# A transformer layer on one core: four of the seven operand sums of the down projection made one stage earlier and stored, the rest moved to VectorE

## The chip, the core and the metric

One core of a Trainium2 chip runs the whole kernel. The metric is the device time in microseconds (us), the median of three timed runs; lower is better. The engines of the core are TensorE (PE, with its weight load PEld), VectorE (DVE), ScalarE (ACT), GpSimd (POOL) and SyncE (SP), which here only issues DMA transfers.

## The reference

The kernel computes one layer of a hybrid encoder in float32 on 1024 tokens with 1024 features: attention and a recurrence side by side, an output projection, and then a SwiGLU block with 2816 hidden features (22 tiles of 128). Only the last line matters here:

```
h2 = rmsnorm(x, norm2_g[l])
x = x + (jax.nn.silu(h2 @ w_gate[l]) * (h2 @ w_up[l])) @ w_down[l]
```

The stage that makes silu(h2 @ w_gate) * (h2 @ w_up) is called the gate/up stage below, and its result g (2816 x 1024). The product g @ w_down is the down stage.

## The kernel before

**Products.** A float32 product runs as three passes: each operand is the exact sum of two rounded parts h and l, and PE adds h*h, l*h and h*l. An operand is split by one ACT instruction (h, a cast, L72) and one DVE instruction (l, a subtraction, L73), each on 128x512 elements. Both stages use Strassen's scheme in Winograd's form: the left matrix A and the right matrix B are cut into 2 x 2 blocks, and seven products P1 to P7 stand in for eight. Some of their operands are sums of blocks: S1 = A21 + A22, S2 = S1 - A11, S3 = A11 - A21, S4 = A12 - S2, T1 = B12 - B11, T2 = B22 - T1, T3 = B22 - B12, T4 = B21 - T2.

**Gate/up stage.** After a first pair of hidden tiles, which is multiplied plainly (`classic`; its products land in g by the DVE instruction of L942), 20 steps follow, g1, u1, g2, ... u10, two for each of ten pairs of hidden tiles. A step is an object `Step`: it has 7 products of 12 matmuls (L931, tiles Pg and Pu). Its `run` calls `after(i)` behind product i, and that makes the operand i of the next step (`make`: the S sums on POOL at L1060 to L1063, then the split on ACT and DVE). Results leave PSUM through ACT copies and DVE additions (L1091, L1102, L1111). Each finished tile of g is stored to DRAM by `spill` (L923, one 512 KB transfer on SP). The weights come by `load_raw` (L901, 512 KB each, tiles graw and uraw). Four PSUM banks serve the g steps and four the u steps, in turn, so a product waits until the result four products before it in its step has been read.

**Down stage.** The list PRODUCTS gives the order of the seven products: P1 (A11, B11), P2 (A12, B21), P7 (S3, T3), P5 (S1, T1), P6 (S2, T2), P3 (S4, B22), P4 (A22, T4). A is g and B is w_down. Each has 11 positions of 12 matmuls (L1334, tile P), 77 slots of 12 matmuls in all. Operand tiles are named by slot and side: d371l is the l part of slot 37's right operand. The splits run two slots ahead (AHEAD = 2). The raw blocks are loaded by `load_d` (L1168), first from within the last step by `end_step`, then by a list of loads behind it. The table SUMS says which engine makes which sum and where it is put: all S sums on POOL, all T sums on DVE (both L1189), each called by `sum_of` from the loop over the slots. A sum takes the place of a block that is not needed any more. At the ends of the products, DVE adds the PSUM banks to running values (L1341) and ACT copies others out. `add` joins values in SBUF, 28 times, on POOL (L1276). The results go out by L1212.

**Order.** A scheduler puts each engine's instructions in a row, and each engine runs its row in that order, waiting at the head for whatever the instruction needs. The order of a row is therefore what the text speaks of.

Of the kernel before, what the change touches and what calls it, by code (L numbers as in the profile page):

```python
# [9 lines left out]
F32 = mybir.dt.float32  # L10
# [24 lines left out]
def hymba_layer(ctx: ExitStack, tc: tile.TileContext, x, norm1_g, w_in, q_norm_g, k_norm_g, b_f,  # L35
                conv_w, conv_b, w_a, b_a, w_x, b_x, lam, attn_out_g, lru_out_g, w_out, norm2_g,
                w_gate, w_up, w_down, out):
    """Float32 products run as three float32r passes: an operand is the exact sum h + l of two
    float32r values (12 bits each), and h*h + h*l + l*h carries the float32 product."""
# [71 lines left out]
    # the gain on all partitions  # L111
# [54 lines left out]
        # nlc = 4 softplus(-lam), so that tanh(nlc * r) = tanh(-log_a / 2)  # L166
# [17 lines left out]
    def atanh(p_t, z, n):  # L184
        """p_t = atanh(z) for |z| <= 1/3"""
# [18 lines left out]
    # hT[half] = (h, l), each [feature, chunk of features, 512 tokens]  # L204
# [36 lines left out]
    def prep(p):  # L241
        """q and k of two heads, feature-major, as h and l"""
# [13 lines left out]
    def load_max(h):  # L256
        """what the maxima need"""
# [13 lines left out]
    def max_steps(h):  # L271
# [18 lines left out]
        def rows(half):  # L290
            # -max of 512 queries, turned into a row of QB
# [21 lines left out]
    with tc.tile_pool(name="pp", bufs=1) as pp:  # L313
# [36 lines left out]
        def proj_A(c, groups, evac, hooks=()):  # L350
            """psum[channel, token] for 128 channels and n tokens from t0 each; groups of (t2, t0, n)"""
# [15 lines left out]
        def proj_B(c, blocks, n, evac, *tags, hooks=()):  # L367
            """psum[token, column] for 128 tokens each"""
# [39 lines left out]
        # block-diagonal gate weights  # L408
# [32 lines left out]
        def lru_gates(t):  # L441
            """the four pieces of the gates"""
# [14 lines left out]
        def lru(t):  # L457
# [3 lines left out]
            # With t = tanh(-log_a / 2): a = 2 / (1 + t) - 1 and sqrt(1 - a^2) = 2 sqrt(t) / (1 + t).  # L461
            # 1 / (1 + t) = (1 + a) / 2 starts from a = exp(log_a) and takes a Newton step.
# [10 lines left out]
            # here i = -u: the scan runs on -h  # L473
# [61 lines left out]
        def log_f():  # L535
            # -log f = max(-z, 0) + log1p(exp(-|z|)) with exp(-|z|) = (1 - t) / (1 + t), t = tanh(|z| / 2)
# [190 lines left out]
    def spread(p, heads):  # L727
        """the inverse denominators of the heads of a pair, on their features"""
# [34 lines left out]
    # the recurrent half of the output projection, in pieces of 128 tokens by 256 columns  # L763
# [28 lines left out]
    # by head: pieces of the output projection, steps that the product with v lags, steps over which the other work is  # L792
    # spread, and the places of vprep and finish_pair in it
# [60 lines left out]
    def mm_out(groups):  # L854
        """psum += att @ w_out for groups of (psum, block, half), one chunk of features after the other"""
# [10 lines left out]
    # Strassen's scheme in Winograd's form, on two tiles of ff by two halves of d (weights: A) and two halves of d by  # L866
    # two halves of the tokens (B): seven products in place of eight. The sums S, T are float32, then split.
    #   S1 = A21 + A22, S2 = S1 - A11, S3 = A11 - A21, S4 = A12 - S2
    #   T1 = B12 - B11, T2 = B22 - T1, T3 = B22 - B12, T4 = B21 - T2
    #   u1 = A11 B11 + S2 T2, u2 = u1 + S3 T3  # L870
    #   C11 = A11 B11 + A12 B21, C12 = u1 + S1 T1 + S4 B22, C21 = u2 + A22 T4, C22 = u2 + S1 T1
    NPR = NFT // 2
    gz = ctx.enter_context(tc.tile_pool(name="gz", bufs=1))
    # a block's h and l: [tile of chunks 0 and 1, tile of chunks 2 and 3], [P, 2, 512] each
# [76 lines left out]
    with tc.tile_pool(name="nz", bufs=1) as nz:  # L951
# [37 lines left out]
        # the order of what follows: products of the first pair of ff tiles, plainly (g, u), the sums (tc, t3), their  # L989
        # splits (s3, t4), the loads (rw) and operands (mk) of the next pair  # L990
# [11 lines left out]

    T1 = slots4("q", "T1")
# [7 lines left out]
    def minus(eng, x, y, u):  # L1011
        """u = x - y of two split blocks"""
# [4 lines left out]
    def minus_sum(eng, x, t, u):  # L1017
        """u = x - t of a split block and a sum"""
# [30 lines left out]
    class Step:  # L1049
        """one weight matrix on one pair of ff tiles; operands in the order of the products"""  # L1050
# [23 lines left out]
        def run(self, after):  # L1074
# [9 lines left out]
            def result(i, j, x, y, tmp):  # L1084
                """the block x + y of the product, into silu(gate) or silu(gate) * up"""
# [48 lines left out]
    # The same scheme over tokens (A: g, two halves of the tokens by two times eleven tiles of ff) and columns  # L1134
    # (B: w_down). A sum takes the place of an operand that is not needed any more:
    #   S1 in A21, S2 in S1, S4 in A12, T1 in B12, T2 in T1, T4 in B21
    ND = NFT // 2
    UNITS = {"hA": 8, "hC": 8, "hB": 4, "hD": 4, "hE": 4, "hF": 4}
    raw = {}

    def places(*tags):
        """places of [P, 512] in slots"""
# [11 lines left out]
    def load_d(nm, k0, pl):  # L1154
        """blocks k0.. of A11, B21 and the like into places, a transfer for those side by side"""
        i, j = int(nm[1]) - 1, int(nm[2]) - 1
        while pl:
# [4 lines left out]
            if nm[0] == "A":  # L1162
# [14 lines left out]
    SUMS = {"S3": (pool, "sub", "A11", "A21", None), "T3": (dve, "sub", "B22", "B12", None),  # L1177
            "S1": (pool, "add", "A21", "A22", "A21"), "T1": (dve, "sub", "B12", "B11", "B12"),
            "S2": (pool, "sub", "A21", "A11", "A21"), "T2": (dve, "sub", "B22", "B12", "B12"),
            "S4": (pool, "sub", "A12", "A21", "A12"), "T4": (dve, "sub", "B21", "B12", "B21")}  # L1180
    sum_d, src_d, ops_d = {}, {}, {}

    def sum_of(nm, k):
        if nm not in SUMS:
            return raw[nm, k]
        if (nm, k) not in sum_d:
            eng, op, x_, y_, to = SUMS[nm]
            u = raw[to, k] if to else temp(f"{nm}{k}")
            (eng.tensor_add if op == "add" else eng.tensor_sub)(out=u, in0=raw[x_, k], in1=raw[y_, k])  # L1189
# [26 lines left out]
    def end_step(i):  # L1216
# [20 lines left out]
        elif i == 5:  # L1237
            load_d("B12", 0, places("r0", "r1", "r2", "r3"))
# [3 lines left out]
    for k, st in enumerate(steps):  # L1242
        def after(i):
            if k + 1 < len(steps):
# [14 lines left out]
    load_x2(0, 0, four)  # L1259
    load_d("A21", 0, places("hA"))  # L1260
    load_d("B22", 0, places("s0", "s1", "s2", "s3"))
    load_d("A21", 8, places("x0"))
    load_d("B12", 8, places("x1"))
    load_d("B22", 8, hb[:3])
    load_d("A21", 10, hb[3:])
    load_d("B12", 10, hf[:1])
    load_d("A22", 0, [(sq2, 1)])
# [7 lines left out]
    def add(x_, b, y_):  # L1275
        pool.tensor_add(out=at(x_, b), in0=at(x_, b), in1=at(y_, b))  # L1276

    for n, (nm, a_, b_, pos) in enumerate(dsteps):
# [4 lines left out]
        if n + AHEAD > 2:  # L1283
            for i in range(2):
                operand(n + AHEAD, i)
        if nm == "P7":
            if pos:
                sum_of("T1", pos - 1)
            if pos in (2, 4, 6):
                load_d("A22", pos - 1, places({2: "v0", 4: "v1", 6: "x2"}[pos]))  # L1290
            if pos == 10:
                load_d("A22", 7, places("hD"))
# [78 lines left out]
```

## Time and profile before

| | us |
|---|---|
| device time, median of 3 runs (lowest, highest) | 1208.71 (1208.33, 1208.89) |
| span of the profiled execution | 1207.5 |
| down stage: first to last matmul in that span | 958 to 1203.7 |
| the 20 steps g1 to u10: first to last matmul | 570 to 958 |

No device time of the profiled execution itself is on record; its span is 1.2 us below the median of the runs, and sums below are made as differences against the span and carried to the median. PE is busy 96% of the span, DVE 68%, ACT 43%, POOL 28%, and the 16 DMA engines move 101 GB/s on the mean. In the page's table of 40 slices of 30 us each, PE's share falls below 9 tenths late in the program:

```profile
PE   8999999999999989999899999999999999877998
DVE  6427759768887676768655545555455567999694
POOL 2000010031010210146442433424232013586390
PEclk9999999999999899999999999999999999889999
```

Each digit is the busy share of one slice in tenths; PEclk is the clock that TensorE was granted, in tenths of full speed.

### The profile page before, as it was taken

Reading aid. Unit: us, or ns where it says so; the run is one execution under the profiler, and the core shown is the slowest. Engines: PE = TensorE matmul, PEld = TensorE weight load, DVE = VectorE, ACT = ScalarE, POOL = GpSimd, SP = SyncE. Lnnn points to the kernel's source line nnn. Section 1 sums busy time; section 2 is a strip of 40 time slices with the busy share of each in tenths; the row PEclk is TensorE's granted clock in tenths of the full one; section 3 lists DMA queues with packets and bytes.
Section 4 is the critical chain, followed back from the end, with each engine's and each line's share of the span. In section 5 each row is a group of like instructions: output and inputs, shape, how many; then the busy total and the mean of one; then the engine's idle time right before and its main releaser. Section 6 shows DMA issues by size and latency. Waiting matters only on the chain.

```text
span 1207.5 us, 16502 instructions
## 1 busy us (share of the span) xinstructions
PE 1153.9 (96%) x6137; PEld 972.7 (81%) x6137; DVE 817.8 (68%) x1285; ACT 519.6 (43%) x931; POOL 342.1 (28%) x264
## 2 busy tenths in 40 slices
PE   8999999999999989999899999999999999877998
PEld 7988999987887777777788888888888887655876
DVE  6427759768887676768655545555455567999694
ACT  7437775325555453523333333333333344323432
POOL 2000010031010210146442433424232013586390
PEclk9999999999999899999999999999999999889999
DMA  6111111146565566521323123231223891200302
GB/s 245 28 53 45 36 36 36 30 91 147 154 154 138 143 173 190 179 88 35 114 70 105 53 87 92 91 105 53 87 87 122 315 329 54 71 0 1 105 27 79
DMA packets 82650, 122.21 MB, mean 101 GB/s; under 512 B 12097, under 2 KB 55209, under 8 KB 82570
## 3 DMA queue, kind: packets, MB, share of 16 engines
q1 hardware_dynamic: 82570, 121.16, 33.3%
q8 instruction: 48, 0.79, 0.3%
q14 instruction: 32, 0.26, 0.1%
HBM read 80.34 MB, written 24.21 MB: 87 GB/s over the span
## 4 chain that ended last, share of the span: by engine, by line
PE 72%; DVE 17%; DMA 3%; issue 3%; POOL 2%; ACT 2%; SPq 0%; POOLq 0%; DVEq 0%; ACTq 0%
PE Pu L931 16%; PE Pg L931 16%; PE P L1334 9%; PE pag L361 4%; PE pbk L377 4%; PE pbv L377 4%; PE pax L361 4%; PE pbq L377 3%; PE o L698 3%; PE fl L783 3%; DVE dr L1189 2%; DMA rb<-rd 2%; PE mx L284 1%; DVE dhC L1189 1%; PE st L676 1%
## 5 line engine op out<-in xcount | busy, mean ns | idle before, releaser
L684 ACT ACTIVATE pt<-st 128x512 f32<-128x512 f32 (+1 forms) x96 | 47.9, 508 | 52.3 <-PE st L679 27.4
L689 DVE TENSOR_TENSOR ringl<-pt,ringh 128x512 fp32r<-128x512 f32 (+2 forms) x96 | 58.2, 621 | 7.0 <-ACT ringh L686 5.6
L287 DVE TENSOR_REDUCE nm<-mx 128x1 f32<-128x512 f32 (+2 forms) x96 | 51.2, 549 | 13.6 <-PE mx L286 7.5
L783 PE MATMUL fl<-worec,rech 128*128 128x256 f32 x256 | 54.6, 295 | 1.1 <-DVE ql L76 0.7
L480 POOL TENSOR_TENSOR sqR<-sqR,i 128x1024 f32<-128x1024 f32 x3 | 7.2, 2400 | 150.8 <-ACT i L479 150.8
L1091 DVE TENSOR_TENSOR g<-pug,Pg 128x512 f32<-128x512 f32 x30 | 20.6, 687 | 39.2 <-PE Pg L931 39.2
L783 PEld LDWEIGHTS fl<-worec,rech 128*128 128x128 f32 x256 | 43.9, 198 | 3.4 <-DVE ql L76 1.1
L650 POOL TENSOR_TENSOR vl<-vn,vh 128x256 fp32r<-128x256 f32 x16 | 12.3, 774 | 114.6 <-ACT vh L649 114.6
L1088 DVE TENSOR_TENSOR puu<-puu,Pu 128x512 f32<-128x512 f32 x30 | 20.5, 684 | 32.6 <-PE Pu L931 32.5
L676 PE MATMUL st<-set 128*128 128x512 f32 (+1 forms) x96 | 36.2, 378 | 3.6 <-ACT pt L684 3.5
L698 PE MATMUL o<-ringh,vh 128*128 128x512 f32 (+1 forms) x96 | 38.0, 396 | 0.0
L783 PE MATMUL fl<-worec,recl 128*128 128x256 f32 x128 | 37.1, 290 | 0.0
L698 PE MATMUL o<-ringl,vh 128*128 128x512 f32 (+1 forms) x96 | 34.9, 364 | 2.1 <-DVE ringl L689 2.1
L1060 POOL TENSOR_TENSOR S1u<-uraw,uraw 128x512 f32<-128x512 f32 x10 | 12.9, 1285 | 83.7 <-DVE ag32l L73 9.3
L1089 DVE TENSOR_TENSOR g<-g,puu 128x512 f32<-128x512 f32 x40 | 36.1, 904 | 0.3
L1092 ACT ACTIVATE g<-g 128x512 f32<-128x512 f32 x40 | 25.3, 633 | 25.4 <-DVE g L1091 24.6
L1060 POOL TENSOR_TENSOR S1g<-graw,graw 128x512 f32<-128x512 f32 x10 | 13.3, 1333 | 78.8 <-DVE au32l L73 9.3
L698 PE MATMUL o<-ringh,vl 128*128 128x512 f32 (+1 forms) x96 | 34.2, 356 | 0.3 <-POOL vl L650 0.3
L81 POOL TENSOR_TENSOR rs<-rs,neghalf 128x1 f32<-128x1 f32 x16 | 9.8, 615 | 78.7 <-DVE rs L80 72.9
L284 PE MATMUL mx<-set,qms 67*128 67x512 f32 (+2 forms) x72 | 26.0, 389 | 2.5 <-DVE nm L287 2.1
L435 DVE SCALAR_TENSOR_TENSOR xc<-xr,vcol,xc 128x1023 f32<-128x1023 f32 (+2 forms) x12 | 15.4, 1279 | 18.5 <-ACT xc L433 18.4
L686 ACT CAST ringh<-pt 128x512 fp32r<-128x512 f32 (+1 forms) x48 | 26.4, 549 | 1.6 <-PE o L698 0.8
(2203 smaller groups left out, 4234.8 us busy)
## 6 DMA issues: line engine op xcount, KB each, us to landing
graw<-in_w_gate_dram SPq DMA_DIRECT2D x22, 512.0 KB
uraw<-in_w_up_dram SPq DMA_DIRECT2D x22, 512.0 KB
gd<-g SPq DMA_DIRECT2D x22, 512.0 KB
xt<-in_x_dram SPq DMA_DIRECT2D x8, 512.0 KB
set<-qh SPq DMA_DIRECT2D x16, 256.0 KB
xp<-in_x_dram SPq DMA_DIRECT2D x32, 128.0 KB
x1d<-xp SPq DMA_DIRECT2D x32, 128.0 KB
set<-kh SPq DMA_DIRECT2D x14, 256.0 KB
```

The costliest lines, as they stand in the source:

```text
L284: pe.matmul(ps[:, :w], qm[:67, qb * P:(qb + 1) * P], kb[:67, j0 * P:j0 * P + w], start=True, stop=not diag)
L287: dve.tensor_reduce(out=nm[:, ch * 8 + qb:ch * 8 + qb + 1], in_=ps[:, :nk], axis=AX.X, op=ALU.max, negate=True)
L361: pe.matmul(ps[g][:, :n], a, r, start=(kc == 0 and m == 0), stop=(kc == KC - 1 and m == 2))
L377: pe.matmul(ps[g][:, :n], a, r, start=(kc == 0 and m == 0), stop=(kc == KC - 1 and m == 2))
L676: pe.matmul(ps[:, off:], s[:, KA, j * P:(j + 1) * P], s[:, QA, qs:qs + N], start=True, stop=False)
L684: act.activation(out=pt[:, off:], in_=ps[:, off:], func=AF.Exp)
L689: dve.tensor_sub(out=pl[:, off:], in0=pt[:, off:], in1=f32(ph[:, off:]))
L698: pe.matmul(ot[:, off:], a[:, j * VW:j * VW + P], r[:, off:], start=(j == 0 and m == 0), stop=(j == jmax and m == 2))
L783: pe.matmul(ps[:, :256], a, r, start=(n == 0), stop=(n == 11))
L931: pe.matmul(ps, a[:, k, :], chunk(b, k), start=first and m == 0, stop=last and m == 11)
L1189: (eng.tensor_add if op == "add" else eng.tensor_sub)(out=u, in0=raw[x_, k], in1=raw[y_, k])
L1334: pe.matmul(ps, x_[:, bs], y_, start=(begin and m == 0), stop=(end and m == 2))
```

## The change

The sums T1 to T4 do not depend on anything that the program computes, only on w_down; S3 depends on g alone. The change makes them for all 11 positions while the gate/up stage runs.

- `load_wd(f)` loads the two row blocks of w_down that position f needs into one tile wd of four 128x512 parts (two transfers of 512 KB), and `sum_wd` makes T1, T3, T2 and T4 in place, four DVE subtractions, then stores the tile (td, 1 MB). There is one buffer for wd. `after` calls `load_wd(k)` behind product 0 of step k and the four sums behind products 3 to 6, for the first 11 steps.
- `spill` makes S3 of position f on DVE and stores it (sd, 256 KB), for the first 11 tiles of g.
- In the down stage T1 to T4 and S3 are loaded like blocks. A22 is loaded whole where B22 was, B22 later, and B12 not at all. A table NEXT says behind which slot a later operand is loaded into the places of which earlier one: T3 into B11's, T1 into B21's, T2 into S3's, B22 into T3's, T4 into T1's.
- S1, S2 and S4 (33 instructions) and the 28 `add` run on DVE. POOL has nothing left to do in the down stage. Of DVE's row there the 44 T sums are gone.
- A smaller scratch area for DMA descriptors (`dynamic_dma_scratch_size`) makes room in SBUF. Removed docstrings change nothing.

PE's row is the same in both kernels. DVE gets 55 instructions more in the gate/up stage, SP 33 transfers for wd and td and 11 for sd.

The diff, cut to its core:

```diff
 def spill(n, i):
-    sp.dma_start(out=gd[2 * n + i], in_=gts[n][i])
+    f, g = 2 * n + i, gts[n][i]
+    sp.dma_start(out=gd[f], in_=g)
+    if f < ND:
+        s3 = tz.tile([P, 512], F32, tag="s3", name=f"s3_{f}", bufs=2)
+        dve.tensor_sub(out=s3, in0=g[:, :512], in1=g[:, 512:])
+        sp.dma_start(out=sd[f], in_=s3)
...
+TD = {"T1": 0, "T3": 1, "T4": 2, "T2": 3}
+def load_wd(f):
+    wds[f] = wd = tz.tile([P, 4, 512], F32, tag="wd", name=f"wd{f}", bufs=1)
+    for i in range(2):
+        rows = slice((ND * i + f) * P, (ND * i + f + 1) * P)
+        sp.dma_start(out=wd[:, 2 * i:2 * i + 2, :], in_=w_down[0, rows, :].rearrange("p (j c) -> p j c", j=2))
+
+def sum_wd(f, m):
+    wd = wds[f]
+    o, a, b = ((0, 1, 0), (1, 3, 1), (3, 3, 0), (2, 2, 3))[m]
+    dve.tensor_sub(out=wd[:, o, :], in0=wd[:, a, :], in1=wd[:, b, :])
+    if m == 3:
+        sp.dma_start(out=td[f], in_=wd)
...
-SUMS = {"S3": (pool, "sub", "A11", "A21", None), "T3": (dve, "sub", "B22", "B12", None),
-        "S1": (pool, "add", "A21", "A22", "A21"), "T1": (dve, "sub", "B12", "B11", "B12"),
-        "S2": (pool, "sub", "A21", "A11", "A21"), "T2": (dve, "sub", "B22", "B12", "B12"),
-        "S4": (pool, "sub", "A12", "A21", "A12"), "T4": (dve, "sub", "B21", "B12", "B21")}
+SUMS = {"S1": ("add", "A21", "A22", "A21"), "S2": ("sub", "A21", "A11", "A21"), "S4": ("sub", "A12", "A21", "A12")}
...
     def after(i):
+        if k < ND:
+            if i == 0:
+                load_wd(k)
+            elif i > 2:
+                sum_wd(k, i - 3)
...
+NEXT = {("P1", 3): (("T3", 0, "B11", 0),), ("P1", 5): (("T3", 4, "B11", 4),), ...
+        ("P5", 0): (("B22", 0, "T3", 0), ("B22", 4, "T3", 4), ("B22", 6, "T3", 6), ("B22", 10, None, 0)),
+        ("P6", 0): (("T4", 0, "T1", 0), ("T4", 8, "T1", 8), ("T4", 10, "T1", 10))}
...
 def add(x_, b, y_):
-    pool.tensor_add(out=at(x_, b), in0=at(x_, b), in1=at(y_, b))
+    dve.tensor_add(out=at(x_, b), in0=at(x_, b), in1=at(y_, b))
...
+    for to, k0, of, m0 in NEXT.get((nm, pos), ()):
+        load_d(to, k0, held[of, m0] if of else [(sq2, 1)])
     if nm == "P7":
-        if pos:
-            sum_of("T1", pos - 1)
-        if pos in (2, 4, 6):
-            load_d("A22", pos - 1, places({2: "v0", 4: "v1", 6: "x2"}[pos]))
```

The scheduler places the added instructions. DVE's row before, from the end of the plain pair into step g1 (g_5899 and g_5900 are g's first two tiles, cu the plain up product, ag and au operands of steps g1 and u1, Pg products of g1):

```order
L942 TENSOR_TENSOR g_5899<-g_5899,cu_6162 128x512
L73 TENSOR_TENSOR ag14l<-S4g_6153,ag14h 128x512
L942 TENSOR_TENSOR g_5900<-g_5900,cu_6220 128x512
L73 TENSOR_TENSOR ag15l<-S3g_6152,ag15h 128x512
L942 TENSOR_TENSOR g_5900<-g_5900,cu_6254 128x512
L73 TENSOR_TENSOR ag16l<-graw_6003,ag16h 128x512
L73 TENSOR_TENSOR au10l<-uraw_6005,au10h 128x512
L1091 TENSOR_TENSOR g_6301<-pug_6299,Pg_6329 128x512
```

The same place of DVE's row in the changed kernel (s_0 and s_1 are S3 of tiles 0 and 1, wd_6325 and wd_6479 the tiles of positions 0 and 1; L1117 is before's L1091):

```order
L73 TENSOR_TENSOR ag14l<-S4g_6155,ag14h 128x512
L927 TENSOR_TENSOR s_0_6199<-g_5899 128x512
L1025 TENSOR_TENSOR wd_6325<-wd_6325 128x512 x4
L947 TENSOR_TENSOR g_5900<-g_5900,cu_6225 128x512
L73 TENSOR_TENSOR ag15l<-S3g_6154,ag15h 128x512
L947 TENSOR_TENSOR g_5900<-g_5900,cu_6259 128x512
L73 TENSOR_TENSOR ag16l<-graw_6005,ag16h 128x512
L927 TENSOR_TENSOR s_1_6288<-g_5900 128x512
L1025 TENSOR_TENSOR wd_6479<-wd_6479 128x512
L73 TENSOR_TENSOR au10l<-uraw_6007,au10h 128x512
L1025 TENSOR_TENSOR wd_6479<-wd_6479 128x512 x3
L1117 TENSOR_TENSOR g_6309<-pug_6307,Pg_6340 128x512
```

Two S3 sums and eight sums of wd, for positions 0 and 1, now stand ahead of the DVE instruction that reads step g1's second product out of its bank.

SP's row in the changed kernel from the store of position 0's sums:

```order
L1027 DMA td<-wd_6325 128x2048
L1019 DMA wd_6479<-in_w_down_dram 128x1024 x2
L924 DMA gd<-g_5900 128x1024
L928 DMA sd<-s_1_6288 128x512
L901 DMA graw_6305<-in_w_gate_dram 128x4x256
L901 DMA uraw_6459<-in_w_up_dram 128x4x256
L1027 DMA td<-wd_6479 128x2048
L1019 DMA wd_6643<-in_w_down_dram 128x1024 x2
L901 DMA uraw_6461<-in_w_up_dram 128x4x256
```

The load of wd_6479 follows the store of wd_6325 out of the same buffer, and the weight loads graw_6305 and uraw_6461 stand behind such loads.

DVE's row before in the down stage, in the products P7 and P5 (T sums, dr, dhC and dx their places):

```order
L1189 TENSOR_TENSOR T_9908<-dhB,dx_9300 128x512
L1189 TENSOR_TENSOR dr_9252<-dr_9252,dhD 128x512
L73 TENSOR_TENSOR d291l<-T_9877,d291h 128x512
L73 TENSOR_TENSOR d300l<-S_9906,d300h 128x512
L1189 TENSOR_TENSOR T_9933<-dhB,dx_9300 128x512
L1189 TENSOR_TENSOR dx_9300<-dx_9300,dhD 128x512 x2
L73 TENSOR_TENSOR d301l<-T_9908,d301h 128x512
```

And in the changed kernel, in P5 (dhA is first A21, then S1, then S2; dk and dq are first A12, then S4):

```order
L1218 TENSOR_TENSOR dhA<-dhA,dhE 128x512
L1218 TENSOR_TENSOR dk_9322<-dk_9322,dhA 128x512
L73 TENSOR_TENSOR d391l<-dhC,d391h 128x512
L73 TENSOR_TENSOR d400l<-dhA,d400h 128x512
L1218 TENSOR_TENSOR dq_9323<-dq_9323,dhA 128x512
L1218 TENSOR_TENSOR dhA<-dhA,dhE 128x512
L73 TENSOR_TENSOR d401l<-dhC,d401h 128x512
L73 TENSOR_TENSOR d410l<-dx_9424,d410h 128x512
```

Between two pairs of splits stand one S2 and one S4, the second of which reads what the first wrote; no T sum is left, and the right operand is split as it was loaded.

## Rows read from the trace of the kernel before

**Rows 1.** Windows: length; PE, PEld, DVE, ACT, POOL busy; granted clock; DMA share; GB/s

```profile
958.00:1012.00 54.00, 54.00 (x240) 44.72 (x239) 33.72 (x49) 22.20 (x39) 6.26 (x5) 1.00 0.71 253
1012.00:1107.00 95.00, 72.58 (x281) 55.32 (x279) 93.91 (x90) 30.03 (x52) 64.84 (x40) 0.93 0.10 34
1107.00:1140.00 33.00, 32.89 (x145) 27.23 (x146) 23.36 (x34) 16.78 (x31) 8.00 (x6) 1.00 0.24 80
1140.00:1180.00 40.00, 37.90 (x160) 29.20 (x159) 39.89 (x29) 15.93 (x29) 38.03 (x23) 1.00 0.12 43
```

**Rows 2.** Chain of waits: start, length, engine, tile, line, instructions

```profile
578.25 18.05 PE Pg L931 x72
...
939.02 19.04 PE Pu L931 x84
958.06 54.19 PE P L1334 x239
```

**Rows 3.** Timeline, end of the down stage: start, length, engine, instruction

```profile
1203.29 0.39 PE L1334 MATMUL P<-d761l,d760h 128*128 128x512 f32 x1
```

**Rows 4.** Waits of PE, 1012 to 1180: total, times, longest

```profile
PE P L1334 <- DVE dhF L1341: 4.4, 1, 4.4
...
PE P L1334 <- DVE d631l L73: 0.2, 1, 0.2
```

**Rows 5.** Groups of VectorE, 1012 to 1107: busy, mean ns, idle before

```profile
L1189 DVE TENSOR_TENSOR dhC<-dhC,dr 128x512 f32<-128x512 f32 x8 | 13.8, 1748 | 0.0
...
L1341 DVE TENSOR_TENSOR dhF<-dhF,P 128x512 f32<-128x512 f32 x6 | 3.7, 673 | 0.0
```

**Rows 6.** Timeline of VectorE in P3

```profile
1107.58 0.68 DVE L1189 TENSOR_TENSOR dhF<-dhB,dhF 128x512 f32<-128x512 f32 x1
1108.29 0.69 DVE L1189 TENSOR_TENSOR dq<-dq,dhF 128x512 f32<-128x512 f32 x1
1108.90 0.68 DVE L73 TENSOR_TENSOR d441l<-dr,d441h 128x512 fp32r<-128x512 f32 x1
```

**Rows 7.** Timeline of SyncE: loads and stores as they were issued

```profile
916.61 0.34 SPq L923 DMA_DIRECT2D gd<-g  x1
920.12 0.37 SPq L1168 DMA_DIRECT2D dx<-in_w_down_dram  x1
...
987.73 0.43 SPq L1168 DMA_DIRECT2D dhF<-in_w_down_dram  x1
...
1029.40 0.38 SPq L1168 DMA_DIRECT2D dv<-gd  x1
...
1048.94 0.36 SPq L1168 DMA_DIRECT2D dhD<-gd  x1
```

**Rows 8.** Timeline of GpSimd: sums that waited for such loads

```profile
1033.17 1.42 POOL L1189 TENSOR_TENSOR dhA<-dhA,dv 128x512 f32<-128x512 f32 x1 [0.87 <-DMA dv<-gd]
...
1054.15 1.42 POOL L1189 TENSOR_TENSOR dhA<-dhA,dhD 128x512 f32<-128x512 f32 x1 [6.43 <-DMA dhD<-gd]
```

**Rows 9.** Timeline of VectorE, first products of step g1

```profile
578.12 1.15 DVE L73 TENSOR_TENSOR ag14l<-S4g,ag14h 128x512 fp32r<-128x512 f32 x1
...
579.80 1.45 DVE L73 TENSOR_TENSOR ag15l<-S3g,ag15h 128x512 fp32r<-128x512 f32 x1
...
583.69 0.67 DVE L1091 TENSOR_TENSOR g<-pug,Pg 128x512 f32<-128x512 f32 x1
```

**Rows 10.** Timeline of PE, second and sixth product of step g1

```profile
578.25 0.79 PE L931 MATMUL Pg<-B21hD,ag11h 128*128 128x512 f32 x1 [3.29 <-DVE g L942]
...
590.70 0.61 PE L931 MATMUL Pg<-T,ag15h 128*128 128x512 f32 x2
```

**Rows 11.** Windows, step u1, columns as in rows 1

```profile
597.00:616.00 19.00, 19.00 (x85) 15.73 (x85) 10.43 (x16) 5.96 (x10) 7.13 (x5) 1.00 0.26 84
```

**Rows 12.** Timeline of GpSimd: first sums of steps g2 and u2

```profile
587.36 1.29 POOL L1060 TENSOR_TENSOR S1g<-graw,graw 128x512 f32<-128x512 f32 x1 [4.74 <-DMA graw<-in_w_gate_dram]
...
605.92 1.28 POOL L1060 TENSOR_TENSOR S1u<-uraw,uraw 128x512 f32<-128x512 f32 x1 [9.25 <-DVE ag22l L73]
```

More of the change, by code (lines that the diff above doesn't have):

```diff
@@ L1001, in temp @@
         return tz.tile([P, 512], F32, tag="sf", name=name, bufs=4)
+    ND = NFT // 2
+    TD = {"T1": 0, "T3": 1, "T4": 2, "T2": 3}
+    td = dr.tile([ND, P, 4, 512], F32, name="td")
+    sd = dr.tile([ND, P, 512], F32, name="sd")
+    wds = {}
+    def load_wd(f):
[9 more added lines that the diff above has]
+            sp.dma_start(out=td[f], in_=wd)
     T1 = slots4("q", "T1")
@@ L1131, in hymba_layer @@
             {"tc": t_chain, "t3": t_3, "s3": split_3, "t4": t_4, "sp": lambda i: spill(0, i)}[q[:2]](int(q[2]))
-    ND = NFT // 2
     UNITS = {"hA": 8, "hC": 8, "hB": 4, "hD": 4, "hE": 4, "hF": 4}
     raw = {}
+    held = {}
     def places(*tags):
@@ L1154, in load_d @@
     def load_d(nm, k0, pl):
-        i, j = int(nm[1]) - 1, int(nm[2]) - 1
+        held[nm, k0] = pl
+        i, j = int(nm[1]) - 1, int(nm[-1]) - 1
         while pl:
@@ L1161, in load_d @@
                 m += 1
-            if nm[0] == "A":
+            if nm in TD:
+                src = td[k0:k0 + m, :, TD[nm], :].rearrange("f p c -> p f c")
+            elif nm == "S3":
+                src = sd[k0:k0 + m].rearrange("f p t -> p f t")
+            elif nm[0] == "A":
                 f0 = ND * j + k0
@@ L1186, in sum_of @@
         if (nm, k) not in sum_d:
-            eng, op, x_, y_, to = SUMS[nm]
-            u = raw[to, k] if to else temp(f"{nm}{k}")
-            (eng.tensor_add if op == "add" else eng.tensor_sub)(out=u, in0=raw[x_, k], in1=raw[y_, k])
+            op, x_, y_, to = SUMS[nm]
+            u = raw[to, k]
+            (dve.tensor_add if op == "add" else dve.tensor_sub)(out=u, in0=raw[x_, k], in1=raw[y_, k])
             sum_d[nm, k] = u
@@ L1237, in end_step @@
         elif i == 5:
-            load_d("B12", 0, places("r0", "r1", "r2", "r3"))
+            load_d("S3", 0, places("r0", "r1", "r2", "r3"))
         if i < 6:
@@ L1259, in hymba_layer @@
     load_x2(0, 0, four)
+    load_d("S3", 8, places("x1"))
+    load_d("S3", 10, hf[:1])
     load_d("A21", 0, places("hA"))
-    load_d("B22", 0, places("s0", "s1", "s2", "s3"))
+    load_d("A22", 0, places("s0", "s1", "s2", "s3"))
     load_d("A21", 8, places("x0"))
-    load_d("B12", 8, places("x1"))
-    load_d("B22", 8, hb[:3])
     load_d("A21", 10, hb[3:])
-    load_d("B12", 10, hf[:1])
-    load_d("A22", 0, [(sq2, 1)])
+    load_d("A22", 8, hb[:3])
+    NEXT = {("P1", 3): (("T3", 0, "B11", 0),), ("P1", 5): (("T3", 4, "B11", 4),), ("P1", 8): (("T3", 6, "B11", 6),),
[5 rows of a table added]
     set0, set1 = A4, B4
@@ L1285, in hymba_layer @@
                 operand(n + AHEAD, i)
+        for to, k0, of, m0 in NEXT.get((nm, pos), ()):
+            load_d(to, k0, held[of, m0] if of else [(sq2, 1)])
         if nm == "P7":
-            if pos:
-                sum_of("T1", pos - 1)
-            if pos in (2, 4, 6):
-                load_d("A22", pos - 1, places({2: "v0", 4: "v1", 6: "x2"}[pos]))
-            if pos == 10:
-                load_d("A22", 7, places("hD"))
             if pos == 4:
@@ L1356 @@
     from concourse.bass_utils import run_bass_kernel_spmd as _run
-    nc = _bacc.Bacc("TRN2", target_bir_lowering=False, num_devices=1)
+    nc = _bacc.Bacc("TRN2", target_bir_lowering=False, num_devices=1, dynamic_dma_scratch_size=2048)
     arrays, args = {}, []
```

3 rows, old and new, of the table NEXT are left out of this document.

## The prediction

> **What bounds the kernel now.** I read the windows first, then the chain of waits, then PE's waits, then single stretches of the timeline. In the chain, each step of the gate/up stage is one unbroken run of 84 matmuls in 19.04 us, 0.2267 us each, and the down stage begins at the same pace: 239 matmuls in 54.19 us from 958.06 [rows 2]. The last matmul ends at 1203.29 + 0.39 = 1203.68 [rows 3]. So the down stage takes 245.6 us, while its 77 x 12 = 924 matmuls at 0.2267 us need 209.5 us, 209.6 with the longer end of the last. **36.0 us** of it are not multiplication at full pace.
>
> The windows say where they lie [rows 1]. From 1012 to 1107 PE is busy 72.6 of 95 us: 22.4 us stand idle, and its 281 matmuls, which would need 63.7 us, take 8.9 us more, at a mean granted clock of 0.93, so partly at 1.2 instead of 2.4 GHz. From 1140 to 1180 it is 2.1 us idle and 1.6 us slow. That is 35.0 of the 36.0 us. PE's waits between 1012 and 1180 are 17 in number, from 4.4 us down to 0.2 us, nearly all for a DVE instruction, most often a split [rows 4]. DVE is busy 93.9 of 95 us there and 39.9 of 40 [rows 1]: it is the bound. It is not short of speed by itself: its 90 instructions take 1.04 us each in that window, whereas in P3, from 1108, where POOL rests, one follows another after 0.61 us, or 0.71 us where it reads what the one ahead wrote (1108.29 to 1108.90, 1107.58 to 1108.29) [rows 6]. Beside POOL (64.8 of 95 us busy, 40 sums [rows 1]) a DVE sum of two SBUF tiles takes 1.75 us, while in the same window one that reads a PSUM tile takes 0.67 us [rows 5]. So POOL's sums slow exactly those DVE instructions whose two inputs are in SBUF.
>
> The Trainium skill ("SBUF — State Buffer", section "SBUF: two separate sides") says the same as a rule: a DVE instruction with two SBUF inputs and a GpSimd instruction that reads SBUF lock a shared port against each other, and the loser waits out the whole instruction. By that rule the trace agrees.
>
> **Part 1: sums gone from POOL and DVE in the down stage.** The 72 POOL instructions go. DVE loses 44 T sums there and gains 33 S sums and 28 adds, 17 more in all, but none of its instructions meets POOL any more. The tightest stretch is P5: per slot two splits, one S2 and one S4, which reads the S2 just made: 3 x 0.61 + 0.71 = 2.54 us, against 12 x 0.2267 = 2.72 us of PE. At 0.60 to 0.61 us that leaves 0.18 us a slot, about 2 us over 11 slots. In P3 and P4 the 28 adds and the readings of PSUM banks come to some 46 instructions in 11 slots where they are densest, 46 x 0.61 / 11 = 2.55 us a slot, again under 2.72. At a boundary DVE has up to four more instructions (2.4 us) in a row, and PE two prepared slots (5.4 us) in hand. I therefore take the whole 36.0 us as gained: no pauses, and so no slow matmuls behind them. Bounds: 36.0 from above, since PE's matmuls are unchanged; from below 33, if the boundaries keep one pause of the smaller size seen, about 1.5 us, and its slow matmuls.
>
> **Part 2: operands that are loaded.** T3 is the first, and it replaces B11 in its places as P1 goes on. P7 starts 22 slots into the stage, 958.1 + 22 x 2.72 = 1017.9, with splits some 5 us ahead, at 1012. The list of blocks ahead of T3 in SP's row holds the same volume as before's list, whose last load was issued at 987.7 [rows 7]; T3's 2.9 MB behind it at the window's 253 GB/s [rows 1] need 11.5 us, and a load of 512 KB landed 3.8 us behind its issue (1029.40 to 1033.17), one of 1 MB 5.2 us (1048.94 to 1054.15) [rows 7, 8]. 987.7 + 11.5 + 5.2 = 1004, 8 us of margin. The later ones (T1, T2, B22, T4) have a whole product, 30 us, each. DMA share is 0.10 to 0.24 there [rows 1]. Cost taken: 0.
>
> **Part 3: the added sums in the gate/up stage.** In a step DVE is busy 10.4 of 19 us [rows 11], and the 55 new instructions are spread over some eight steps at 5 to 7 each, 3.3 to 5 us of the 8.6 us that stand free. As work they are hidden. What counts is that each position's sums wait for a round trip through the one buffer wd, at the head of DVE's row, with everything else of DVE queued behind. A store of 512 KB held the load behind it for 3.51 us (916.61 to 920.12) [rows 7]; for the store of 1 MB I add the difference of the two loads, 1.44 us: 4.95. With 3.77 us for the next load, the round trip is **8.7 us**.
>
> Its first instance is in step g1, which has no lead. Behind ag14l, which ended at 579.2, DVE now makes S3 of tile 0 (beside a POOL sum, like ag15l's 1.45 us: to 580.6) and four sums at 0.66 (to 583.2), all ahead of the last readings of the plain products [rows 9]. The store is issued at 583.3, so the next position's data are there at 592.0. Then come one sum, one split and three sums (0.6 to 0.7 each, to 595.2), and only then the DVE instruction that ran at 583.69 before and that frees the bank of step g1's second product [rows 9]: 595.9. PE's sixth product takes that bank and started at 590.70 [rows 10]; now 596.0, **+5.3 us**. After its last pause, of 3.29 us, PE needed 18.05 us for 72 matmuls [rows 2, 10] in place of 16.3: **+1.7 us** at the lower clock. Sum +7.0 us. The 1.4 us or so that the first group of sums delays the third product lie within it.
>
> The later nine round trips, into step g8, hold DVE too, but they stand further from what PE needs next: a bank is read one to four products (2.7 to 10.9 us) ahead of its reuse, and operands are made one step (19 us) ahead. On SP, weight loads wait behind a load of wd, some 5 to 7 us. In before the first sums of g2 came at 587.36, of u2 at 605.92 [rows 12], each with 28 us or so until PE starts the step's products, so that is covered. I take 0 for all nine. Bounds for part 3: with two transfers of 512 KB as the round trip (7.3 us) and no clock price, +3.8; with two 1 MB transfers (10.4 us) +8.7 us with the clock, and some 10 if step u1 is held up a little as well. No gain is possible, since PE has no pause in these steps to give back.
>
> The rule of the shared port would speak against this part: if each of the five added sums of step g1's first group lost 1.1 us to a POOL sum, the result would be 5.5 us later. Only the first of them has a POOL sum beside it in the trace, and I keep to that.
>
> **Sum.** 1207.5 - 36.0 + 7.0 = 1178.5 for the profiled span; on the median, 1.2 us above it: 1208.7 - 29.0 = **1179.7 us**.
>
> **Rivals.** (a) *DVE stays the bound in the down stage*. If an instruction takes the 0.69 us of its own length [rows 6] instead of 0.61 from start to start, P5 needs 3 x 0.69 + 0.71 = 2.78 us a slot, and the dense part of P3 and P4 46 x 0.69 / 11 = 2.89: over PE by 0.06 and 0.17 us for 11 slots each, 2.5 us, and with pauses come two stretches of slow clock, 3.4 us, so about 1186. For it: a slack of only 7%. Against: rows 6 show 0.61. (b) *T3's loads come late*: if the loads around 958 to 1000, which now include the T's places being emptied, run 12 us behind, PE waits some 12 - 8 = 4 us at P7, and again after it for T1; with the slow clock about 1188 to 1193. For it: the stage opens with DMA at 0.71 [rows 1]. (c) *Slower than before*: the round trip stops PE in the later positions too. The place is the head of DVE's row in steps u1 to g8; the price is up to the 7.0 us of the first, the number is ten; from 36.0 / 10 = 3.6 us each the gain is gone, and at 6 stops of 7.0 us the time is 1208.7 - 36.0 + 42 = 1214.7. For it: one buffer, and nothing else to run on DVE meanwhile. Against: 8.6 us free of 19 and the banks' lead. (d) *It does not do what it says*: DVE's long instructions are not POOL's doing, so the down stage keeps its time; then 1208.7 + 7.0 = 1215.7. Rows 5 and 6 speak against it.
>
> **How the numbers follow.** A difference under 0.2% (2.4 us) cannot be told from none. Forecast 0.68 (1173 to 1186: part 3 at 3.8 and everything won gives 1176.5, or less if even the first stop is hidden, 1172.7; part 3 at 10 and part 1 at 33 gives 1185.7). Rival (a) 0.10, (b) 0.09, (c) 0.07, (d) 0.03, and a mixture that lands within 0.2% 0.03. Faster 0.87, same 0.03, slower 0.10. The range reaches from 1173 to 1193, where forecast, (a) and (b) lie; outside are (c), (d) and the mixture, and a little of (b).
>
> **What would show it.** Right: POOL at 0 in the down stage; DVE's sums there at 0.6 to 0.7 us; the chain of waits with one unbroken run of PE over some 209.5 us; in step g1 a wait of PE for DVE's reading of a bank, about 5 us, and a first wd sum that waits for its load. Wrong: PE waiting for a split's l part in P5 or P4 (a), for a load of T3 or T1 (b), DVE idle at wd with PE idle behind it in steps u1 to g8 (c), DVE sums of 1.7 us without POOL (d).

## The result, and the profile after

The changed kernel takes **1189.4 us** (median of 4 runs, 1187.19 to 1192.0) against 1208.52 us of the kernel before (4 runs, 1208.09 to 1208.89): 0.9838 of its time, with a 95% interval of 0.9821 to 0.9854. Forecast were 1179.7 us and 29 us gained; 19 us came. The profiled execution took 1189.54 us, with a span of 1187.8 us.

Two stretches tell the story, and they are read separately. First the down stage: the chain of waits (start, length, engine, tile, line, instructions), the last matmul, and the windows of that stage (columns as in [rows 1]).

```profile
974.70 207.41 PE P L1371 x915
```

```profile
1183.75 0.39 PE L1371 MATMUL P<-d761l,d760h 128*128 128x512 f32 x1
```

```profile
966.00:1010.00 44.00, 44.00 (x196) 36.45 (x195) 26.36 (x42) 16.81 (x30) 1.31 (x1) 1.00 0.98 356
1010.00:1050.00 40.00, 40.00 (x178) 33.13 (x177) 26.44 (x43) 19.15 (x34) 0.00 (x0) 1.00 0.80 276
1050.00:1100.00 50.00, 50.00 (x222) 41.42 (x221) 42.95 (x69) 22.94 (x41) 0.00 (x0) 1.00 0.29 97
1100.00:1140.00 40.00, 40.00 (x178) 33.12 (x177) 28.98 (x48) 18.75 (x34) 0.00 (x0) 1.00 0.25 79
```

One run of 915 of the stage's 924 matmuls with no wait in it, where before there were 17 waits [rows 4] and a window 22 us idle [rows 1]. POOL is at 0 from 1010, DVE's instructions take 0.60 to 0.63 us each (42.95 us for 69) in place of 1.04, the granted clock is 1.00 in all four windows. From 974.70 to 1184.14 the stage takes 209.4 us, against 245.6: 36.2 us won.

Now the gate/up stage. Its first product began at 568.47, 1.9 us earlier than before; the instructions of PE, DVE, ACT and POOL up to there stand in the same order in both kernels, and in the profiles of the runs below that start lies anywhere from 568.5 to 575.5, so that is taken as the execution's own scatter. The stage then lasted 974.70 - 568.47 = 406.2 us, against 958.06 - 570.36 = 387.7: **18.5 us lost**. Added up, 36.2 - 18.5 + 1.9 = 19.6 us, and the spans differ by 19.7. PE's waits of the stage for L1117 (total, times, longest), PE's timeline at its stops (in brackets the idle time ahead and who ended it), and three windows:

```profile
PE Pg L936 <- DVE g L1117: 10.6, 4, 3.9
```

```profile
582.52 0.74 PE L936 MATMUL Pg<-T,ag12h 128*128 128x512 f32 x2 [1.54 <-DVE g L947]
594.93 1.22 PE L936 MATMUL Pg<-T,ag15h 128*128 128x512 f32 x2 [3.91 <-DVE g L1117]
...
677.36 0.73 PE L936 MATMUL Pg<-T,ag35h 128*128 128x512 f32 x2 [3.13 <-DVE g L1117]
...
718.80 0.73 PE L936 MATMUL Pg<-T,ag45h 128*128 128x512 f32 x2 [3.06 <-DVE g L1117]
...
759.52 0.73 PE L936 MATMUL Pg<-T,ag55h 128*128 128x512 f32 x2 [0.48 <-DVE g L1117]
```

```profile
578.00:597.00 19.00, 13.54 (x50) 10.39 (x49) 13.57 (x20) 2.71 (x6) 2.53 (x3) 0.86 0.76 266
...
673.00:692.00 19.00, 15.87 (x70) 12.81 (x69) 14.17 (x21) 5.80 (x11) 7.07 (x5) 1.00 0.60 208
...
711.00:730.00 19.00, 15.94 (x63) 12.65 (x63) 13.03 (x20) 3.51 (x7) 5.90 (x5) 0.91 0.62 229
```

Four times it is the sixth product of a g step that waits for the DVE instruction that reads the second product out of its bank: in g1, as forecast, but also in g3, g4 and g5. What each step lost shows in its length, from its first matmul to that of the next step. Step g1 before, then g1, g3 and g4 in the changed kernel:

```profile
570.36 0.73 PE L931 MATMUL Pg<-B,ag10h 128*128 128x512 f32 x2 [1.91 <-DVE g L942]
...
596.14 0.61 PE L931 MATMUL Pu<-B,au10h 128*128 128x512 f32 x2
```

```profile
568.47 0.74 PE L936 MATMUL Pg<-B,ag10h 128*128 128x512 f32 x2 [1.91 <-DVE g L947]
...
603.15 0.61 PE L936 MATMUL Pu<-B,au10h 128*128 128x512 f32 x2
...
660.46 0.61 PE L936 MATMUL Pg<-B,ag30h 128*128 128x512 f32 x2
...
682.93 0.62 PE L936 MATMUL Pu<-B,au30h 128*128 128x512 f32 x2
...
701.97 0.62 PE L936 MATMUL Pg<-B,ag40h 128*128 128x512 f32 x2
...
726.01 0.62 PE L936 MATMUL Pu<-B,au40h 128*128 128x512 f32 x2
```

Step g1 took 34.7 us in place of 25.8 (+8.9), g3 22.5 in place of 19.04 (+3.4), g4 24.0 in place of 19.04 (+5.0); g5 lost 0.8, u2 and u4 0.2 each, together 18.5. In g3 nearly all of it is the stop itself: behind it 70 matmuls in 15.87 us are 0.2267 us each, full pace. The stop of the same length in g4 was followed by matmuls below full pace: 63 in 15.94 us, where full pace is 14.3, at a granted clock of 0.91.

Why DVE is late is in its own rows: the group of the 44 added sums of w_down (count, busy, mean ns, idle ahead of them and what ended it), then DVE's timeline in g1 and before the stop in g4.

```profile
L1025 DVE TENSOR_TENSOR wd<-wd 128x512 f32<-128x512 f32 x44 | 43.6, 992 | 39.7 <-DMA wd<-in_w_down_dram 39.1
```

```profile
577.93 3.94 DVE L1025 TENSOR_TENSOR wd<-wd 128x512 f32<-128x512 f32 x4
...
589.73 0.69 DVE L1025 TENSOR_TENSOR wd<-wd 128x512 f32<-128x512 f32 x1 [4.15 <-DMA wd<-in_w_down_dram]
...
592.13 2.15 DVE L1025 TENSOR_TENSOR wd<-wd 128x512 f32<-128x512 f32 x3 [1.11 <-DMA wd<-in_w_down_dram]
594.20 0.68 DVE L1117 TENSOR_TENSOR g<-pug,Pg 128x512 f32<-128x512 f32 x1
...
703.75 0.69 DVE L1025 TENSOR_TENSOR wd<-wd 128x512 f32<-128x512 f32 x1 [7.10 <-DMA wd<-in_w_down_dram]
...
705.02 2.39 DVE L1025 TENSOR_TENSOR wd<-wd 128x512 f32<-128x512 f32 x2
...
709.13 1.77 DVE L1025 TENSOR_TENSOR wd<-wd 128x512 f32<-128x512 f32 x1
...
713.35 1.67 DVE L1115 TENSOR_TENSOR g<-g,puu 128x512 f32<-128x512 f32 x1
...
718.06 0.68 DVE L1117 TENSOR_TENSOR g<-pug,Pg 128x512 f32<-128x512 f32 x1
```

The 44 sums stood 39.1 us waiting for wd with DVE's whole row behind them, and took 0.99 us each on the mean, not 0.66. A wait of 7.1 us from the end of step u3 to 703.75, in g4, and three instructions of 1.7 us beside POOL's sums put DVE so far back that it read the bank of g4's second product only at 718.06.

### The profile page after: what moved, and what is told of

Same layout as the page of the kernel before. It is cut to its first block, busy times and chain, and to the rows that moved or that the text cites. A ratio compares the mean times of both kernels' runs of the same rounds, so it can differ in the third digit from the quotient of the medians.

```text
span 1187.8 us, 16586 instructions
## 1 busy us (share of the span) xinstructions
PE 1146.5 (97%) x6137; PEld 971.1 (82%) x6137; DVE 812.5 (68%) x1357; ACT 514.6 (43%) x931; POOL 228.4 (19%) x192
## 4 chain that ended last, share of the span: by engine, by line
PE 70%; DVE 14%; DMA 9%; issue 3%; ACT 2%; POOL 1%; SPq 1%; DVEq 0%; POOLq 0%; ACTq 0%
PE P L1371 17%; PE Pu L936 10%; PE Pg L936 8%; DMA wd<-in_w_down_dram 4%; PE pag L361 4%; PE pbk L377 4%; PE pbv L377 4%; PE pax L361 4%; PE pbq L377 3%; PE o L698 3%; PE fl L783 3%; DVE wd L1025 3%; DMA td<-wd 2%; PE mx L284 1%; PE st L676 1%
## 5 line engine op out<-in xcount | busy, mean ns | idle before, releaser
L1025 DVE TENSOR_TENSOR wd<-wd 128x512 f32<-128x512 f32 x44 | 43.6, 992 | 39.7 <-DMA wd<-in_w_down_dram 39.1
L1117 DVE TENSOR_TENSOR g<-pug,Pg 128x512 f32<-128x512 f32 x30 | 20.5, 684 | 27.4 <-PE Pg L936 18.8
L435 DVE SCALAR_TENSOR_TENSOR xc<-xr,vcol,xc 128x1023 f32<-128x1023 f32 (+2 forms) x12 | 15.4, 1280 | 18.5 <-ACT xc L433 18.4
L861 PE MATMUL wa<-wah,atth 128*128 128x512 f32 x64 | 26.0, 406 | 1.0 <-ACT wah L72 1.0
```

The costliest lines, as they stand in the source:

```text
L1025: dve.tensor_sub(out=wd[:, o, :], in0=wd[:, a, :], in1=wd[:, b, :])
```

## The experiments

Theory A: the down stage was held up by POOL's sums beside DVE's, and the gate/up stage now loses its 18.5 us in DVE's row, at sums that stand too early and wait for wd. The rivals are named in the expectations. e1 to e4 ran on one chip, e5 to e8 on a second; the kernel before took 1208.42 us (1206.06 to 1214.62) on the first and 1208.84 us (1206.34 to 1213.99) on the second. Ratios are to that kernel on the same chip; the changed kernel's, for comparison, is 0.9838.

**e1: the sums of w_down left out, every transfer kept.**

```diff
-        dve.tensor_sub(out=wd[:, o, :], in0=wd[:, a, :], in1=wd[:, b, :])
```

> Leaves out the 44 sums of w_down (wd is loaded and stored as it came, so the down stage multiplies raw blocks); every transfer stays. Theory A: the changed kernel loses its 18.5 us in the gate/up stage (568.5 to 974.7 in its trace, 387.7 us in the kernel before) in VectorE's row alone, where the sums stand ahead of readings of PSUM banks and wait for wd. Then the stage takes some 388 us again and the time is 1189.4 - 17 to 18.5, about 1171 to 1173. Rival B: the 26 MB more of transfers, and the weight loads queued behind them on SyncE, cost it; then most of the loss stays, 1185 or more.

1175.0 us (1172.77 to 1176.92), ratio 0.9718 (0.9686 to 0.9749). The chain of waits runs from step g1's second product to the end of the stage without a piece that is not PE:

```profile
580.86 17.98 PE Pg L936 x72
...
960.60 207.41 PE P L1370 x915
```

960.60 - 580.86 = 379.7 us, as in the kernel before (958.06 - 578.25 = 379.8 [rows 2]). The transfers alone cost nothing, and rival B falls. The median is 2 us above the expectation; in the execution profiled (1175.44 us) that lies ahead of the stage, whose second product began 4.5 us later than the changed kernel's (580.86, there 576.37).

**e2: the sums pinned where the program is written.**

```diff
-        dve.tensor_sub(out=wd[:, o, :], in0=wd[:, a, :], in1=wd[:, b, :])
+        tc.keep_in_program_order(dve.tensor_sub(out=wd[:, o, :], in0=wd[:, a, :], in1=wd[:, b, :]))
```

> All sums are made, but each is pinned in VectorE's row at the place where the program is written (position k's sums behind products 3 to 6 of step k), so none runs ahead of a PSUM reading that its step needs. Theory A (waiting at the head of the row, brought about by the early place): the stops in steps g1, g3 and g4 go, 1172 to 1177. Rival C (the 44 instructions themselves, slowed by GpSimd's sums beside them, 0.99 us each in the changed kernel's trace, overfill VectorE): the loss stays, 1185 or more. In between if round trips are longer than the 8 to 11 us that the places leave.

1180.33 us (1177.4 to 1184.94), ratio 0.9762 (0.9717 to 0.9808): half of the loss goes, half stays (578.49 to 967.24 is 388.7 us, 8.9 more than before). The stops of g1, g3 and g5 are gone, one of 2.2 us in g4 is left, and PE stops in u5 and u6. PE's stops, an instruction of DVE ahead of that in u5, and the sums' group:

```profile
707.72 0.91 PE L936 MATMUL Pg<-T,ag45h 128*128 128x512 f32 x2 [2.19 <-DVE g L1117]
...
765.96 0.74 PE L936 MATMUL Pu<-B,au54h 128*128 128x512 f32 x2 [1.60 <-ACT puu L1124]
...
806.45 0.73 PE L936 MATMUL Pu<-B,au64h 128*128 128x512 f32 x2 [1.72 <-ACT puu L1124]
```

```profile
758.17 0.69 DVE L1025 TENSOR_TENSOR wd<-wd 128x512 f32<-128x512 f32 x1 [3.80 <-DMA wd<-in_w_down_dram]
```

```profile
L1025 DVE TENSOR_TENSOR wd<-wd 128x512 f32<-128x512 f32 x44 | 38.3, 871 | 44.9 <-DMA wd<-in_w_down_dram 44.9
```

Still 44.9 us of waiting for wd: a sum that is behind every reading of its own step is still ahead of those of the next, and the last sum of a position comes too late in a step for the next position's data to be there. In u5 it is ACT that reads a bank late, but ACT had waited 7.5 us, to 761.98, for a DVE instruction behind the sum of 758.17. That speaks for the round trip, but does not yet exclude rival C.

**e5: the sums pinned, one position every 1.7 steps.** (wd's loads and stores are pinned in SP's row as well.)

```diff
...
-            if k < ND:
+            f = {(17 * j) // 10 + 1: j for j in range(ND)}.get(k)
+            if f is not None:
                 if i == 0:
-                    load_wd(k)
+                    load_wd(f)
                 elif i > 2:
-                    sum_wd(k, i - 3)
+                    sum_wd(f, i - 3)
```

> As e2, but position k's sums stand in step 1 + 1.7 k instead of step k, so that nearly always a store and a load have a whole step more. e2 still lost some 9 us in the gate/up stage. If that is the round trip of the one buffer (VectorE idle at wd for 44.9 us in e2, theory A), it goes: the stage takes 388 to 390 us, 1172 to 1176. If it is GpSimd's sums beside the added instructions (rival C), it stays or spreads: 1179 or more.

**1172.94 us** (1172.37 to 1174.74), ratio 0.9694 (0.9667 to 0.9722). The group of the sums, and the chain:

```profile
L1025 DVE TENSOR_TENSOR wd<-wd 128x512 f32<-128x512 f32 x44 | 39.4, 895 | 13.2 <-DMA wd<-in_w_down_dram 13.1
```

```profile
579.85 18.25 PE Pg L936 x72
...
959.86 207.41 PE P L1372 x915
```

The same 44 sums at nearly the same length (0.90 us, so beside POOL as before) and 13.1 us of waiting: 380.0 us from g1's second product, no stop. At this pace fewer sums fall into a step, which would help rival C as well; but from 597 to 806 DVE was busy 145.2 us here and 150.7 us in e2, nearly as much, and in neither near the 209 us of that stretch. So the loss was the waiting, at that place and pace; the lengthened instructions are hidden once it is gone, and rival C falls as a cause of its own. Whether the pins in SP's row had a share beside the pace, no run shows.

**e3 and e6: the kernel before, with all its sums and adds on VectorE and nothing else changed.**

```diff
-    SUMS = {"S3": (pool, "sub", "A11", "A21", None), ...
-            "S1": (pool, "add", "A21", "A22", "A21"), ...
-            "S2": (pool, "sub", "A21", "A11", "A21"), ...
-            "S4": (pool, "sub", "A12", "A21", "A12"), ...
+    SUMS = {"S3": (dve, "sub", "A11", "A21", None), ...
+            "S1": (dve, "add", "A21", "A22", "A21"), ...
+            "S2": (dve, "sub", "A21", "A11", "A21"), ...
+            "S4": (dve, "sub", "A12", "A21", "A12"), ...
...
-        pool.tensor_add(out=at(x_, b), in0=at(x_, b), in1=at(y_, b))
+        dve.tensor_add(out=at(x_, b), in0=at(x_, b), in1=at(y_, b))
```

> The kernel before with one part of the change alone: all S and T sums and the 28 adds on VectorE, made in the down stage as before, nothing stored or loaded more; GpSimd idle there. Theory A (GpSimd's sums slow VectorE's, the number of instructions is second): 90 + 40 instructions of the window 1012 to 1107 at 0.61 to 0.65 us are 80 to 85 us against 95 us, and the later stretch fits under PE: 12 to 18 us faster than before, 1190 to 1197. Rival D (VectorE's 1.04 us are its own): 130 x 1.04 = 135 us, 40 us slower than before, about 1248.

> The kernel of e3 once more, beside the kernel before on the same chip: 0.97 of its time as in e3, 1172 to 1178, faster than the changed kernel.

**1176.37 us** (1172.08 to 1177.7) and **1174.33 us** (1172.39 to 1175.41), ratios 0.9724 (0.9689 to 0.9758) and 0.9706 (0.9681 to 0.9731): five edited lines, no table of loads and no stored sum, and faster than the change. It also beats the expectation, by 14 to 21 us. The chain and two windows of e3:

```profile
956.68 207.41 PE P L1334 x915
```

```profile
1016.00:1046.00 30.00, 30.00 (x134) 24.86 (x133) 30.00 (x51) 14.91 (x26) 0.00 (x0) 1.00 0.24 79
...
1106.00:1136.00 30.00, 30.00 (x134) 24.86 (x133) 30.00 (x51) 13.19 (x24) 0.00 (x0) 1.00 0.18 65
```

DVE has 72 instructions more than before in the down stage and does one every 0.59 us. From 1010 to 1136 it is busy 125.8 of 126 us, and PE beside it is never late. The expectation put all 130 instructions that DVE and POOL had in the window 1012 to 1107 into one stretch, 80 to 85 us, longer than the 63.7 us that PE needs for that window's matmuls. But a good part may be sums for products still to come, which can run later: DVE was full up to 1136 where before it had 9.6 us free between 1107 and 1140 [rows 1]. That this is the reason is argued from the windows, not tested by itself. Rival D falls altogether.

**e4: the changed kernel, with S1, S2, S4 and the adds back on GpSimd.**

```diff
-            (dve.tensor_add if op == "add" else dve.tensor_sub)(out=u, in0=raw[x_, k], in1=raw[y_, k])
+            (pool.tensor_add if op == "add" else pool.tensor_sub)(out=u, in0=raw[x_, k], in1=raw[y_, k])
...
-        dve.tensor_add(out=at(x_, b), in0=at(x_, b), in1=at(y_, b))
+        pool.tensor_add(out=at(x_, b), in0=at(x_, b), in1=at(y_, b))
```

> The changed kernel with S1, S2, S4 and the adds of the down stage back on GpSimd; T1 to T4 and S3 still loaded. Theory A: a GpSimd sum costs VectorE about 1 us where they meet (before: 90 x 0.61 + 40 x 1 = 95 us), so P5 needs 2 x 0.61 + 2 x 1 = 3.2 us a slot and GpSimd itself 2 x 1.7 = 3.4, over PE's 2.72: 5 to 12 us slower than the changed kernel, 1194 to 1201. Rival E (it was the 44 T sums leaving VectorE that counted, GpSimd does no harm): 1189, as the changed kernel.

1199.5 us (1197.6 to 1205.15), ratio 0.9929 (0.9897 to 0.9961), some 11 us slower than the changed kernel. DVE has 61 instructions fewer than there, and they take 1.06 us again in this window:

```profile
1060.00:1130.00 70.00, 68.27 (x295) 54.58 (x294) 60.16 (x57) 31.95 (x57) 43.89 (x28) 1.00 0.25 84
```

Taking instructions from DVE and giving them to POOL made the down stage longer, 218.3 us (973.98 to 1192.3) in place of 209.4. Rival E falls: GpSimd does harm. But half of it stands: the stage is 27.3 us shorter than the 245.6 of the kernel before, with S1, S2, S4 and the adds on POOL in both. Taking the 44 T sums off DVE and the 11 S3 sums off POOL is worth that much as long as POOL works beside DVE.

**e7 and e8: e3's kernel with unrelated GpSimd work beside it.** In e7, 44 additions of two tiles that nothing else uses; in e8, 44 memsets of one (e8 has `pool.memset(dm[:, 0, :], 1.0)` for the addition; both have the change's smaller descriptor scratch area, to make room for dm).

```diff
+    dm = tz.tile([P, 3, 512], F32, tag="dm", name="dm")
+    pool.memset(dm, 0.0)
...
+        if 20 <= n < 64:
+            pool.tensor_copy(out=dm[:, 0, :1], in_=f32(ops_d[n + AHEAD, 0][0])[:, :1])
+            tc.keep_in_program_order(pool.tensor_add(out=dm[:, 0, :], in0=dm[:, 1, :], in1=dm[:, 2, :]))
```

> e3's kernel, and on GpSimd 44 additions of two unrelated SBUF tiles of 128x512, one for each of slots 22 to 65 (released by a 128x1 copy out of that slot's h part, which holds up nothing else). No other row changes. Theory A: each takes about 1.1 us from VectorE, which e3 leaves no idle time from 1010 to 1136; 44 x 1 = 44 us, some of it within its slack after slot 55, and slow matmuls behind the pauses: 1205 to 1225. Rival F (the former loss was order and dependence between the two engines, not the instructions meeting): 1176.

> As e7, with a memset of 128x512, which reads nothing, in place of each addition. If only GpSimd instructions that read SBUF hold VectorE up, the time stays with e3: 1172 to 1179. If any GpSimd write of that size does, it is as slow as e7.

e7: 1216.62 us (1214.74 to 1222.59), ratio 1.0069 (1.0043 to 1.0095), a little slower than the kernel before. e8: 1174.35 us (1173.1 to 1176.64), ratio 0.9710 (0.9684 to 0.9736), as e3. Nothing waits for the additions or the memsets. ACT waits four times for one of the 128x1 copies ahead of them, 10.7 us in all in e7 and 7.3 us in e8, where it costs nothing. So the 42 us between the two are the meeting itself, but for what a few us more of that wait may have cost; 42 of DVE's instructions in e7 take over 1 us, none in e8's down stage does. POOL's and DVE's timelines of e7 over the same stretch:

```profile
1051.43 1.61 POOL L1290 TENSOR_TENSOR dm<-dm 128x512 f32<-128x512 f32 x1
...
1053.71 1.63 POOL L1290 TENSOR_TENSOR dm<-dm 128x512 f32<-128x512 f32 x1
```

```profile
1051.23 0.68 DVE L73 TENSOR_TENSOR d310l<-S,d310h 128x512 fp32r<-128x512 f32 x1
1051.83 1.76 DVE L73 TENSOR_TENSOR d311l<-T,d311h 128x512 fp32r<-128x512 f32 x1
1053.52 0.68 DVE L1189 TENSOR_TENSOR dr<-dr,dhD 128x512 f32<-128x512 f32 x1
1054.12 1.78 DVE L73 TENSOR_TENSOR d320l<-S,d320h 128x512 fp32r<-128x512 f32 x1
```

POOL's addition runs from 1051.43 to 1053.04. The DVE split issued at 1051.83 ends at 1053.59, 0.55 us behind POOL's end, about the 0.59 us that one takes of a full row in e3: as if it did its whole work after POOL was through. The next one is undisturbed, the one after meets POOL's next addition. And e8, POOL and DVE:

```profile
1053.24 0.53 POOL L1290 MEMSET dm<- 128x512 f32 x1
```

```profile
1053.06 0.69 DVE L73 TENSOR_TENSOR d370l<-dhA,d370h 128x512 fp32r<-128x512 f32 x1
```

A memset of the same size in the middle of a split changes nothing. The Trainium skill ("SBUF — State Buffer", section "SBUF: two separate sides") words it as an exclusive lock between a DVE instruction with two SBUF inputs and a GpSimd instruction that reads SBUF; these rows agree in both halves, 1.76 us against 0.69.

## Why the prediction was right, and where it was not

**What bounds the kernel: right.** DVE, slowed by POOL. e7 shows it without a sum of the one that the other needs; e3 shows that DVE has room for 72 instructions more once POOL rests, and e4 that its count of instructions does matter while POOL works beside it.

**Part 1, the down stage: right to 0.2 us.** 36.0 us were forecast, 36.2 came, with no wait and full clock. But the reason given was only half needed. The sum set P5's 2.54 us per slot against 2.72 and so took the missing T sums as what made room; e3 has them all back and PE does not wait. Of the change, the move from POOL to DVE is worth the 36 us by itself, and the stored sums nothing on top of it (without the move, e4, they are worth 27.3): e5, the change with its loss mended, and e6, before with the move alone, differ by less than their runs scatter (1172.37 to 1174.74, and 1172.39 to 1175.41).

**Part 2, the loads: right.** No wait of PE for a loaded operand, though DMA was at 0.98 up to 1010.

**Part 3, the gate/up stage: the mechanism right, the size wrong.** 7.0 us forecast, 18.5 measured. In g1 the chain of steps held: the store was issued at 581.89, and PE's sixth product came at 594.93 instead of 590.70 although the stage had begun 1.9 us earlier, so 6.1 us late for the forecast 5.3. The clock fell (0.86 from 578 to 597), and from there to the end of the step PE took 8.2 us in place of 5.4, 2.8 us more for the forecast 1.7. The step lost 8.9 us for the forecast 7.0.

The step that failed is "I take 0 for all nine": behind g1, steps g3, g4 and g5 lost 3.4, 5.0 and 0.8 us, u2 and u4 0.2 each, 9.6 us in all. Two numbers behind that zero were off. The added sums were taken at 0.6 to 0.7 us; they took 0.99 on the mean, since POOL makes the next step's sums beside them, the very effect that the same prediction counted on in the down stage. The rule of the shared port was weighed for g1 and kept for one instruction. There it held: one of the first four sums of wd met a POOL sum and took 1.76 us, the others 0.69 each. But it was not carried on to the later steps, and 14 of the 44 sums took over 1 us. And 8.6 us free of 19 in a step is a mean over a row that runs in order: sums and S3 (55 at about 1 us over eight steps, 6.8 us a step) and waits for wd (39.1 over eight, 4.9 us) come to 11.7 us. That sum is an estimate, since DVE may have had nothing else to run during a part of a wait. So DVE fell behind until a reading of a bank came late; e5 shows that of the two it was the waits that had to go.

That the time lies within the range is in part luck. The range reaches up to 1193 for (a) and (b), which did not occur; the forecast's own bounds end at 1186. What brought the time to 1189.4 was the place and mechanism of (c), whose time the prediction put outside the range.

**The rivals.** (c) was half right: its place and mechanism are what happened, but at four stops and not six, and behind the first at 0.8 to 5.0 us a step. Its "u1 to g8" is too long: by `k < ND` the last position's sums belong to step g6, and the last of them ran at 746.65, in g5. (a), (b) and (d) did not occur.

## What to carry to other kernels

Before instructions are moved out of a full stage, see what each takes there and what it takes alone: a sum that is 0.6 us by itself and 1.7 us beside another engine can call for moving the other engine's work, even onto the full engine: alone that made the whole of the gain here (e3, e6). Work put into an engine's free time brings its waits with it: in a row that runs in order, a wait for a transfer at a badly chosen place costs everything behind it, so put it behind the readings that a product needs and leave a whole step for the round trip. A share of idle time says neither whether an instruction's neighbours slow it nor whether the idle time lies where the wait falls.

## What the runs showed of the hardware that was not expected

A GpSimd memset of 128x512 (0.53 us) does not touch VectorE, while an addition (1.6 us) holds up a VectorE instruction with two SBUF inputs until it ends (1.76 us in place of 0.69). VectorE keeps up one 128x512 float32 sum every 0.59 us for 126 us on end (e3, 51 in 30 us), each 0.68 to 0.71 us long by itself. And a stop of PE of 3.1 us was followed by matmuls at 0.2267 us in g3, and by longer ones in g4 (granted clock 0.91 in the window); in e2 a stop of 2.2 us was followed by 24 matmuls in 7.36 us, where full pace is 5.4 (granted clock 0.92 from 692 to 711). What a stop costs beyond itself could not be read off its length here.
